# A hybrid decoder trunk on one core: attention operands in 128-row operations placed by two transfers in a row, logits copied with values, one norm step moved ahead, and one weight granule taken off priority

## The chip, the core and the metric

The kernel runs on one core of one Trainium2 chip. The metric is the device time of one execution in microseconds (us). Three runs of the kernel before took 1808.95, 1806.12 and 1806.35 us; the median is 1806.35 us. The kernel works throughout on fp32 data, 512 tokens (T) of width 1024.

## The reference, cut to what matters

```python
for l in range(DEPTH):                                    # DEPTH = 2
    x = x + 0.5 * swiglu(rms_norm(x, ffn1_norm[l]), ffn1_w_in[l], ffn1_w_out[l])
    h = rms_norm(x, mix_norm[l]) @ w_mix_in[l]
    (c_x, c_b, c_c, h_q, h_f, h_i, h_g, f_q, f_k, f_v, f_f) = jnp.split(h, split_at, axis=-1)
    y = jnp.concatenate([
        short_conv_mixer(c_x, c_b, c_c, conv_w[l]),       # 256 channels
        hgrn2_mixer(h_q, h_f, h_i, h_g, lower_bounds[l], hgrn_out_gain[l]),   # 4 heads of 64
        fox_mixer(f_q, f_k, f_v, f_f, fox_f_bias[l], fox_q_gain[l], fox_k_gain[l]),  # 8 heads of 64
    ], axis=-1)
    x = x + y @ w_mix_out[l]
    x = x + 0.5 * swiglu(rms_norm(x, ffn2_norm[l]), ffn2_w_in[l], ffn2_w_out[l])
```

In `fox_mixer` queries and keys are RMS-normed per head; the score of query t and key s gets `c_t - c_s`, where c is the running sum of `log_sigmoid(f_f + f_bias)`; then a causal mask, a softmax and the product with the values. In `hgrn2_mixer` the output of the recurrence is RMS-normed per head and multiplied by a gate.

## The kernel before

**Products in parts.** Each fp32 product is made of three matmuls on a high and a low part of both operands (`mm3`, L322, L330, L331). Weights stream through `granule`: SyncE issues the load of a tile `st` (L294, two buffers), ScalarE casts it to the high part of a tile `hl` (L311), VectorE subtracts to get the low part (L312; three `hl` buffers). These two casts normally have high priority in the scheduler, which puts the instructions of each engine into one order by priorities and readiness. An engine runs its instructions strictly in that order.

**PSUM.** There are eight banks: three called mm, two sc, two pt, one po. A tile of a name waits until the readers of the tile that had the bank before it are done.

**The mixing stage** (`mix`, L1023, once a layer) projects, then runs three mixers beside each other. The last projection before the recurrence gives the HGRN values and the eight forgetting logits in one product 264 wide, in four banks of 128 tokens: ScalarE copies 256 columns to `v` (L1122), VectorE makes the logits `zf` from the other 8 (L1125), four of each. The generator `hgrn` ends with its norm: two matmuls sum squares into two pt banks (`mb`, L1463), then come Ln, Exp and Square on ScalarE, and a Newton step of which the first two VectorE operations (L1473, `T<-pt,T`, one per half of the tile) read the two banks again and so give them back. L1476 to L1485 finish the output `hy`.

**Attention.** `fox_prep` makes a head's operands: four TensorE transposes (L1560) bring 64 query rows and 64 key rows into one bank; for the heads 0 and 1 it is an sc bank, for all others a pt bank. The score is a product over 128 + 66 rows: KA with QA, and KB with QB. QA holds the high query part in rows 0 to 63 and the low one in rows 64 to 127; KA holds the high key part in both halves; QB holds the high query part and two rows of ones, KB the low key part and two rows of the sums c. ScalarE writes QA's upper half (L1563) and KA's lower half (L1564), SyncE copies QB from QA and KA from KA (L1565, L1566, 64 rows, 128 KB each), VectorE writes QA's lower half (L1567) and KB (L1571). GpSimd fills QB's ones (L1557), SyncE loads KB's sums (L1556).

`fox_attend` goes over the items (head, query block i). `scores` runs three items ahead (`LOOK`): two matmuls into an sc bank (L1586, L1587), a custom VectorE operation for mask and maximum (L1591), Exp, reciprocal (L1595), scaling (L1597; L1599 on VectorE for i = 2). Then the block P is transposed into a pt bank (L1651); ScalarE casts it to PH (L1653), VectorE subtracts to PL (L1654); `values` multiplies (L1609) into the po bank, which L1622 and L1623 empty. Head h+1 is prepared at item (h, 0), ahead of that item's scores; each half of four heads prepares its own first head when it starts. Heads 0 to 3 run beside the projections of the convolution (L322 `mm<-x,hl`), heads 4 to 7 beside the first part of the output projection (`most`: `hy`, `cyh`, `fyh`). The rest of the output projection (three of eight rows of tiles, in two groups `dg`) follows; in each group the first granule is 128x1024.

The times below are of layer one; layer two runs the same program about 892 us later.

Of the kernel before, what the change touches and what calls it, by code (L numbers as in the profile page):

```python
# [8 lines left out]
F32 = mybir.dt.float32  # L9
F32R = mybir.dt.float32r  # L10
# [3 lines left out]
AF = mybir.ActivationFunctionType  # L14
# [9 lines left out]
P = 128  # L24
# [133 lines left out]
class Trunk:  # L158
# [177 lines left out]
        for _ in self.stream_steps(*args, **kw):  # L336
            pass

    def stream_steps(self, jobs, parts_of, act, nk, mid=None, pre=None, given=None, queued=False, ending=None):
        k = 0  # L340
        while k < nk:
            kk = min(2, nk - k)
            if callable(mid) and k == nk - 2:
                mid()
            if pre is not None:
                pre(k)
            end = k + kk == nk
            if end and ending is not None:
                jobs = ending
            skew = SKEW_MOVING if jobs[0][2] is not None and jobs[-1][0].shape[-1] < T else 0  # L350
            keep = given is not None and given(k)
            rows = self.granule(
                parts_of(k, kk), kk, pre is None, skew, keep, queued, queued and k == 0
            )
            if keep:
                yield
            order = (
                [(job, j) for job in jobs for j in range(kk)]
                if end
                else [(job, j) for j in range(kk) for job in jobs]  # L360
            )
            for n, ((acc, cols, toks, *more), j) in enumerate(order):
                if pre is not None and n == len(order) // 2:
# [659 lines left out]
    def mix(self, l, w, w_out, conv_w, out_gain, q_gain, k_gain, f_bias, next_gain):  # L1023
# [3 lines left out]
        with tc.tile_pool(name=self.n("mix"), bufs=1) as mp:  # L1027
# [88 lines left out]
                [(bv[i][:, :264], slice(0, 264), TOK[i]) for i in range(4)],  # L1116
                cols((H_I, 256), (F_F, 8)), self.xact, KD,
            )
            v = hp.tile([P, 4, 256], F32, tag="v", name=self.n("v"))
            zf = mp.tile([P, 4, NH], F32, tag="zf", name=self.n("zf"))  # L1120
            for i in range(4):
                nc.scalar.activation(  # L1122
                    v[:, i, :], bv[i][:, :256], AF.Copy, scale=self.invc[:, i : i + 1]
                )
                nc.vector.scalar_tensor_tensor(  # L1125
                    out=zf[:, i, :], in0=bv[i][:, 256:264], scalar=self.invc[:, i : i + 1],
                    in1=fb, op0=ALU.mult, op1=ALU.add,
                )
            half = [{}, {}]

            def projections():
# [6 lines left out]
            for part, n in enumerate(hgrn):  # L1138
                if n is None:
                    break  # L1140
                if n == 0:
                    left.close()
                    ap1 = left.enter_context(
                        tc.tile_pool(name=self.n("at"), bufs=1, reuse_waits="tile")
                    )
                    for tag in ("PH", "PL"):
                        ap1.tile([P, 4, 2, P], F32R, tag=tag, name=self.n(tag), bufs=2)
                    ops = {h: self.fox_prep(ap1, h, half[0][0], qkg, "sc") for h in range(2)}
                if part < 2:
# [3 lines left out]
            attend = self.fox_attend(ap1, 0, half[0], qkg, ops)  # L1153
            next(attend)
            for _ in dense:
                pass
# [41 lines left out]
            def rows(k0, a, n):  # L1198
                return lambda k, kk: [
                    w_out[order[k0 + k] * P : (order[k0 + k] + kk) * P, a : a + n]  # L1200
                ]
# [15 lines left out]
                        add(2 * dg + i, banks[i])  # L1217

            beside(attend, conv(), 1, finish)
            beside(self.fox_attend(ap1, 1, half[1], qkg, {}), most())  # L1220
            self.ntog = 0
            for dg in range(2):
                banks = self.next4()
                self.stream(
                    [(bk, c, None) for bk, c in zip(banks, TOK)],
                    rows(5, 512 * dg, 512), act(5), 3,
                )
                for i in range(4):
                    j = 4 * dg + i
                    add(j, banks[i])  # L1230
                    self.norm_part(j, ap2)
# [33 lines left out]
    def hgrn(self, l, hp, hb, z, q, v, sg, og):  # L1265
# [202 lines left out]
        for x in range(2):  # L1468
            self.act(span(r, x), mb[x], AF.Ln, bias=self.epsc)
        self.act(r, r, AF.Exp, scale=-0.5)  # L1470
        self.act(t, r, AF.Square)
        for x in range(2):
            nc.vector.scalar_tensor_tensor(  # L1473
                out=span(t, x), in0=mb[x], scalar=EPS, in1=span(t, x), op0=ALU.add, op1=ALU.mult
            )
        nc.vector.tensor_scalar(t, t, scalar1=-0.5, scalar2=1.5, op0=ALU.mult, op1=ALU.add)  # L1476
        nc.vector.tensor_mul(r, r, t)
        nc.vector.tensor_mul(o, o, r)
# [70 lines left out]
                )  # L1549
        half[hf] = qk, V  # L1550

    def fox_prep(self, pool, h, qk, g, tag="pt"):
        nc = self.nc
        tl = lambda p, tag: pool.tile([p, T], F32R, tag=tag, name=self.n(tag), bufs=2)
        QA, QB, KA, KB = tl(P, "QA"), tl(66, "QB"), tl(P, "KA"), tl(66, "KB")
        nc.sync.dma_start(KB[64:66, :].bitcast(F32), self.negc[h : h + 1, :, :].bitcast(F32))  # L1556
        nc.gpsimd.memset(QB[64:66, :].bitcast(F32), 1.0)  # L1557
# [6 lines left out]
        nc.scalar.activation(KA[64:, :], b[64:, :], AF.Copy, scale=g[64:, :])  # L1564
        nc.sync.dma_start(QB[:64, :].bitcast(F32), QA[:64, :].bitcast(F32))  # L1565
# [8 lines left out]
        )  # L1574
        return QA, QB, KA, KB

    def fox_attend(self, pool, hf, qkv, g, ops):
        nc = self.nc
        qk, V = qkv
# [52 lines left out]
        if heads[0] not in ops:  # L1632
            ops[heads[0]] = self.fox_prep(pool, heads[0], qk, g)
# [239 lines left out]
```

## Time and profile before

| | |
|---|---|
| runs, us | 1808.95, 1806.12, 1806.35 |
| median, us | 1806.35 |
| profiled execution, us | 1808.44 |
| its span, us | 1806.7 |
| TensorE (PE) busy | 1795.8 us, 99% |
| VectorE (DVE) busy | 1453.4 us, 80% |
| ScalarE (ACT) busy | 1000.7 us, 55% |
| GpSimd (POOL) busy | 170.4 us, 9% |
| granted TensorE clock | full in all 40 slices |

The profiled execution is 1.74 us longer than its span and 2.1 us longer than the median. A row of the timeline gives the start, the time to the modelled end and, in brackets, the idle time ahead of it with the instruction that ended it. Matmuls overlap in the pipeline, so that a row's second column is longer than what the matmul costs; what TensorE loses is read from the distance of two starts. VectorE's and ScalarE's rows overlap a little in the same way.

### The profile page before, as it was taken

What the parts mean: (1) busy time and instruction counts of PE and PEld (TensorE: products, weight loads), DVE (VectorE), ACT (ScalarE), POOL (GpSimd) and SP (SyncE); (2) the same over time, 40 slices, a digit from 0 to 9 for tenths busy, and PEclk for the clock granted to TensorE, in tenths of its full rate; (3) what the DMA queues carried; (4) which work ended last, traced back from release to release, by engine and by line L of the source; (5) the groups of instructions that cost most, each with busy time, mean ns of one, the idle gap of its engine ahead of it and who ended that gap; (6) DMA issues with size and microseconds to landing.
All of it is one profiled execution on the core that took longest, in us unless ns stands there. A gap on an engine that the chain in (4) does not pass through costs nothing.

```text
span 1806.7 us, 34748 instructions
## 1 busy us (share of the span) xinstructions
PE 1795.8 (99%) x14267; PEld 1681.3 (93%) x14267; DVE 1453.4 (80%) x2036; ACT 1000.7 (55%) x1437; POOL 170.4 (9%) x172
## 2 busy tenths in 40 slices
PE   9999999999999999999999999999999999999999
PEld 7899999899888899999889999998998888999997
DVE  8889787776887898879679887876868878888893
ACT  5455554464786465556446555555547855555551
POOL 0011120100000001112001111201000000020210
PEclk9999999999999999999999999999999999999999
DMA  7668783233323767868265787823333247687762
GB/s 203 182 142 186 178 178 98 72 79 83 88 74 111 218 140 161 198 160 169 82 205 133 165 189 191 169 66 81 78 89 89 71 138 188 164 159 192 159 134 94
DMA packets 243486, 250.94 MB, mean 139 GB/s; under 512 B 18520, under 2 KB 228192, under 8 KB 243328
## 3 DMA queue, kind: packets, MB, share of 16 engines
q1 hardware_dynamic: 189424, 182.38, 33.8%
q0 software_dynamic: 53600, 66.09, 23.2%
q8 instruction: 112, 1.84, 0.4%
q14 instruction: 46, 0.38, 0.1%
q10 hardware_dynamic: 304, 0.27, 0.0%
HBM read 223.98 MB, written 2.10 MB: 125 GB/s over the span
## 4 chain that ended last, share of the span: by engine, by line
PE 92%; DVE 3%; ACT 3%; issue 1%; DMA 1%; SPq 0%; ACTq 0%; DVEq 0%
PE mm L322 13%; PE mm L330 13%; PE mm L331 13%; PE sc L330 6%; PE sc L331 6%; PE sc L322 6%; PE pt L322 6%; PE pt L330 6%; PE pt L331 6%; PE po L330 4%; PE po L322 4%; PE po L331 4%; ACT hl L311 1%; PE po L1609 1%; PE pt L1651 1%
## 5 line engine op out<-in xcount | busy, mean ns | idle before, releaser
L803 ACT CAST hl<-w 128x1024 fp32r<-128x1024 f32 x322 | 336.7, 1050 | 313.7 <-PE mm L331 82.4
L805 DVE TENSOR_TENSOR hl<-w,hl 128x1024 fp32r<-128x1024 f32 x322 | 392.2, 1221 | 80.7 <-ACT hl L803 80.7
L312 DVE TENSOR_TENSOR hl<-st,hl 128x512 fp32r<-128x512 f32 (+3 forms) x192 | 162.3, 845 | 106.3 <-ACT hl L311 105.5
L311 ACT CAST hl<-st 128x512 fp32r<-128x512 f32 (+3 forms) x192 | 142.6, 743 | 169.9 <-PE po L331 64.6
L322 PE MATMUL mm<-xc,hl 128*128 128x256 f32 (+1 forms) x733 | 201.2, 276 | 0.0
L330 PE MATMUL mm<-xc,hl 128*128 128x256 f32 x728 | 201.2, 276 | 0.0
L331 PE MATMUL mm<-xc,hl 128*128 128x256 f32 x728 | 201.0, 276 | 0.0
L322 PE MATMUL sc<-xc,hl 128*128 128x256 f32 (+1 forms) x532 | 146.0, 276 | 0.0
L330 PE MATMUL sc<-xc,hl 128*128 128x256 f32 x528 | 146.0, 276 | 0.0
L331 PE MATMUL sc<-xc,hl 128*128 128x256 f32 x528 | 145.9, 276 | 0.0
L322 PEld LDWEIGHTS mm<-xc,hl 128*128 128x128 f32 x733 | 137.4, 188 | 0.2
L330 PEld LDWEIGHTS mm<-xc,hl 128*128 128x128 f32 x728 | 136.7, 188 | 0.0
L331 PEld LDWEIGHTS mm<-xc,hl 128*128 128x128 f32 x728 | 136.7, 188 | 0.0
L322 PE MATMUL pt<-xc,hl 128*128 128x256 f32 (+1 forms) x482 | 132.6, 276 | 0.0
L330 PE MATMUL pt<-xc,hl 128*128 128x256 f32 x480 | 132.6, 276 | 0.0
L331 PE MATMUL pt<-xc,hl 128*128 128x256 f32 x480 | 132.5, 276 | 0.0
L322 PE MATMUL mm<-x,hl 128*128 128x512 f32 x272 | 107.4, 395 | 0.0
L331 PE MATMUL mm<-x,hl 128*128 128x512 f32 x272 | 106.4, 391 | 0.0
L330 PE MATMUL mm<-x,hl 128*128 128x512 f32 x272 | 106.1, 390 | 0.0
L322 PEld LDWEIGHTS sc<-xc,hl 128*128 128x128 f32 x532 | 99.7, 188 | 0.2
L331 PEld LDWEIGHTS sc<-xc,hl 128*128 128x128 f32 x528 | 99.1, 188 | 0.1
L330 PEld LDWEIGHTS sc<-xc,hl 128*128 128x128 f32 x528 | 99.2, 188 | 0.0
(513 smaller groups left out, 5594.1 us busy)
## 6 DMA issues: line engine op xcount, KB each, us to landing
w<-in_ffn_w_in_dram SPq DMA_DIRECT2D x140, 512.0 KB
w<-in_ffn_w_out_dram SPq DMA_DIRECT2D x64, 512.0 KB
w<-in_ffn_w_out_dram POOLq DMA_DIRECT2D x56, 512.0 KB, 8.3
st<-in_w_mix_in_dram SPq DMA_DIRECT2D x88, 256.0 KB
st<-in_ffn_w_in_dram SPq DMA_DIRECT2D x70, 256.0 KB
w<-in_ffn_w_in_dram POOLq DMA_DIRECT2D x35, 512.0 KB, 8.5
w<-S POOLq DMA_DIRECT2D x35, 512.0 KB, 4.7
st<-in_ffn_w_out_dram SPq DMA_DIRECT2D x24, 512.0 KB
```

What stands on the lines that cost most here:

```text
L311: a = nc.scalar.copy(hi, src[:, c : c + w])
L312: b = nc.vector.tensor_sub(lo, src[:, c : c + w], hi)
L322: i = nc.tensor.matmul(acc[:, c], ah, bh[:, c], start=first and c.start == 0, stop=False, skip_group_check=True,)
L330: nc.tensor.matmul(acc, a, b, start=False, stop=False, skip_group_check=True)
L331: i = nc.tensor.matmul(acc, c, d, start=False, stop=last, skip_group_check=True)
L803: A(nc.scalar.copy(hi, src))
L805: return lambda: V(nc.vector.tensor_sub(lo, src, hi))
L1609: nc.tensor.matmul(self.ob[:, t0 + u * P : t0 + 2 * P], V[:, j, h % 4].rearrange("p a d -> p (a d)"), part[:, j, u:, :].rearrange("p i t - ...
L1651: nc.tensor.transpose(tb[:, j * P : (j + 1) * P], p[:, j * P : (j + 1) * P], self.ident)
```

## The change

It has five parts.

1. `v` is 264 wide. ScalarE copies the logits with the values, and one VectorE addition makes all of `zf`.
2. Heads 2 to 7 are prepared in a new way: ScalarE writes 128 rows (KA) in one operation, VectorE 128 rows (QA) in one. Each then holds one half where it belongs and one that belongs elsewhere; SyncE moves the high queries to QB and the low keys to KB, and then GpSimd's queue moves KA's lower half to its upper half and QB's rows into QA's lower half. The second pair needs the first. Heads 0 and 1 keep the old way. QB is two tiles that stay, whose ones are filled once a layer.
3. Head h+2 is prepared at item (h, 0), after that item's scores; so the heads 4 and 5 are prepared while the first half runs.
4. Square and the two operations that read `mb` get high priority.
5. The first granule of the last stream (`dg` 0) loses it (`calm`), and is cast in two pieces.

```diff
@@ stream_steps
-                parts_of(k, kk), kk, pre is None, skew, keep, queued, queued and k == 0
+                parts_of(k, kk), kk, pre is None and not (calm and k == 0), skew, keep,
+                queued, queued and k == 0,
@@ mix
-            v = hp.tile([P, 4, 256], F32, tag="v", name=self.n("v"))
+            v = hp.tile([P, 4, 264], F32, tag="v", name=self.n("v"))
...
-                    v[:, i, :], bv[i][:, :256], AF.Copy, scale=self.invc[:, i : i + 1]
-                )
-                nc.vector.scalar_tensor_tensor(
-                    out=zf[:, i, :], in0=bv[i][:, 256:264], scalar=self.invc[:, i : i + 1],
-                    in1=fb, op0=ALU.mult, op1=ALU.add,
-                )
+                    v[:, i, :], bv[i][:, :264], AF.Copy, scale=self.invc[:, i : i + 1]
+                )
+            nc.vector.tensor_add(
+                zf, v[:, :, 256:264], fb.unsqueeze(1).to_broadcast([P, 4, NH])
+            )
...
+                    self.qb = pair(ap1, "QB", F32R)
+                    for t in self.qb:
+                        nc.gpsimd.memset(t[64:66, :].bitcast(F32), 1.0)
...
-                    rows(5, 512 * dg, 512), act(5), 3,
+                    rows(5, 512 * dg, 512), act(5), 3, calm=dg == 0,
@@ hgrn
-        self.act(t, r, AF.Square)
-        for x in range(2):
-            nc.vector.scalar_tensor_tensor(
-                out=span(t, x), in0=mb[x], scalar=EPS, in1=span(t, x), op0=ALU.add, op1=ALU.mult
-            )
+        with self.tc.high_priority():
+            self.act(t, r, AF.Square)
+            for x in range(2):
+                nc.vector.scalar_tensor_tensor(
+                    out=span(t, x), in0=mb[x], scalar=EPS, in1=span(t, x),
+                    op0=ALU.add, op1=ALU.mult,
+                )
@@ fox_prep
+        if second is not None:
+            row = lambda a, x: a[64 * x : 64 * x + 64, :].bitcast(F32)
+            nc.scalar.activation(KA, b, AF.Copy, scale=g)
+            nc.vector.scalar_tensor_tensor(
+                out=QA, in0=b, scalar=g, in1=KA, op0=ALU.mult, op1=ALU.subtract
+            )
+            nc.sync.dma_start(row(QB, 0), row(KA, 0))
+            nc.sync.dma_start(row(KB, 0), row(QA, 1))
+            second.dma_start(row(KA, 0), row(KA, 1))
+            second.dma_start(row(QA, 1), row(QB, 0))
+            return QA, QB, KA, KB
@@ fox_attend
-            if i == 0 and h + 1 in heads and h + 1 not in ops:
-                ops[h + 1] = self.fox_prep(pool, h + 1, qk, g)
...
+            if i == 0 and h + 2 < NH:
+                ops[h + 2] = self.fox_prep(
+                    pool, h + 2, half[(h + 2) // 4][0], g, second=nc.gpsimd
+                )
```

Lines behind the change move down by up to 16 (L1473 becomes L1477, L1560 L1565, L1586 L1602, L1591 L1607, L1609 L1625, L1651 L1666, L1654 L1669).

**The norm's end on VectorE**, layer one. Before, the first operation that reads an `mb` bank (`T<-pt`) stands behind two of the four low parts of V, and the second behind the mask-and-maximum of the next block (`P,nm<-sc`) and a PL:

```order
L312 TENSOR_TENSOR hl_5573<-st_5570,hl_5573 128x512
L1546 SCALAR_TENSOR_TENSOR V_5246<-mm_5247,invc_3890,V_5246 128x4x64
L1546 SCALAR_TENSOR_TENSOR V_5246<-po_5248,invc_3890,V_5246 128x4x64
L1473 SCALAR_TENSOR_TENSOR T_5544<-pt_5376,T_5544 128x512
L1546 SCALAR_TENSOR_TENSOR V_5246<-mm_5247,invc_3890,V_5246 128x4x64
L312 TENSOR_TENSOR hl_5608<-st_5605,hl_5608 128x512
L1546 SCALAR_TENSOR_TENSOR V_5246<-po_5248,invc_3890,V_5246 128x4x64
L1591 ISA P_5476,nm_5474<-sc_5471,zm_3700 128x512
L1591 ISA nm_5474 128x1
L1654 TENSOR_TENSOR PL_5482<-pt_5483,PH_5481 128x128
L1473 SCALAR_TENSOR_TENSOR T_5544<-pt_5377,T_5544 128x512
```

With the change both stand ahead of V, with one granule's low part between them:

```order
L1607 ISA P_5404,nm_5402<-sc_5399,zm_3700 128x384
L1607 ISA nm_5402 128x1
L1611 RECIPROCAL rs_5383<-rs_5383 128x1
L1611 RECIPROCAL rs_5393<-rs_5393 128x1
L1477 SCALAR_TENSOR_TENSOR T_5556<-pt_5373,T_5556 128x512
L312 TENSOR_TENSOR hl_5585<-st_5582,hl_5585 128x512
L1477 SCALAR_TENSOR_TENSOR T_5556<-pt_5374,T_5556 128x512
L1611 RECIPROCAL rs_5403<-rs_5403 128x1
L1551 SCALAR_TENSOR_TENSOR V_5243<-mm_5244,invc_3890,V_5243 128x4x64
L1615 TENSOR_SCALAR P_5404<-P_5404,rs_5403 128x384
```

Behind these, head 2's new operation (`QA<-pt,qkg,KA`) has joined VectorE, after the rest of V and the mask-and-maximum:

```order
L312 TENSOR_TENSOR hl_5620<-st_5617,hl_5620 128x512
L1551 SCALAR_TENSOR_TENSOR V_5243<-mm_5244,invc_3890,V_5243 128x4x64
L1551 SCALAR_TENSOR_TENSOR V_5243<-po_5245,invc_3890,V_5243 128x4x64
L1607 ISA P_5473,nm_5471<-sc_5468,zm_3700 128x512
L1607 ISA nm_5471 128x1
L1571 SCALAR_TENSOR_TENSOR QA_5478<-pt_5482,qkg_3704,KA_5479 128x512
L1669 TENSOR_TENSOR PL_5494<-pt_5495,PH_5493 128x128
```

So the reads of `mb` moved ahead of all of V, and a whole head's preparation came in behind them; before, it stood some 50 TensorE rows later.

**TensorE at the same place.** Before, the scores of head 0 (its last) and head 1 (its first), then the transpose of the first block P, then the convolution's projection:

```order
L1586 MATMUL sc_5471<-KA_5286,QA_5284 128x512
L1587 MATMUL sc_5471<-KB_5287,QB_5285 128x512
L1586 MATMUL sc_5487<-KA_5303,QA_5301 128x128
L1587 MATMUL sc_5487<-KB_5304,QB_5302 128x128
L1651 MATMUL pt_5483<-ident,P_5387 128x128
L322 MATMUL mm_5451<-x_383_3562,hl_5505 128x512
```

With the change head 2's four transposes (L1565) go ahead of P's; they take the first of the two pt banks that `mb` held, and P's transpose the second:

```order
L1602 MATMUL sc_5468<-KA_5286,QA_5285 128x512
L1603 MATMUL sc_5468<-KB_5287,QB_5281 128x512
L1565 MATMUL pt_5482<-ident,qk_4132 128x128 x4
L1666 MATMUL pt_5495<-ident,P_5384 128x128
L1602 MATMUL sc_5499<-KA_5301,QA_5300 128x128
L1603 MATMUL sc_5499<-KB_5302,QB_5282 128x128
```

Twelve projection matmuls later the next P transpose (`pt_5509`, x2) takes the bank that head 2's transposes fill.

**TensorE where the halves meet**, layer one. Before, head 4 is prepared when the first half is nearly done, right behind the last P transposes of head 3, and head 5 directly after; the scores of head 4 come some 20 rows later:

```order
L1651 MATMUL pt_6044<-ident,P_5991 128x128 x4
L1560 MATMUL pt_6070<-ident,qk_4812 128x128 x4
L322 MATMUL mm_6159<-cyh_3698,hl_6203 128x512
L1609 MATMUL po_6039<-PH_6031,V_4603 128x256
L330 MATMUL mm_6159<-cyl_6017,hl_6203 128x512
```

With the change the heads 4 and 5 have been prepared, and at that place stand the transposes of head 6 in two pieces, with head 4's third and fourth scores among them:

```order
L1666 MATMUL pt_6067<-ident,P_5999 128x128 x4
L1565 MATMUL pt_6131<-ident,qk_4809 128x128 x2
L1602 MATMUL sc_6107<-KA_5828,QA_5827 128x384
L1603 MATMUL sc_6107<-KB_5829,QB_5281 128x384
L1602 MATMUL sc_6117<-KA_5828,QA_5827 128x512
L1625 MATMUL po_6062<-PH_6054,V_4600 128x256
L1603 MATMUL sc_6117<-KB_5829,QB_5281 128x512
L1565 MATMUL pt_6131<-ident,qk_4809 128x128 x2
```

So the scores of the second half moved ahead of the output projection's `cyh` products. GpSimd's queue has twelve transfers more a layer and six fills fewer; SyncE's queue has the same number of transfers.

More of the change, by code (lines that the diff above doesn't have):

```diff
@@ L337, in stream, with stream_steps @@
             pass
-    def stream_steps(self, jobs, parts_of, act, nk, mid=None, pre=None, given=None, queued=False, ending=None):
+    def stream_steps(self, jobs, parts_of, act, nk, mid=None, pre=None, given=None, queued=False, ending=None, calm=False):
         k = 0
@@ L1152, in mix @@
                     next(dense, None)
-            attend = self.fox_attend(ap1, 0, half[0], qkg, ops)
+            attend = self.fox_attend(ap1, 0, half, qkg, ops)
             next(attend)
@@ L1219, in mix @@
             beside(attend, conv(), 1, finish)
-            beside(self.fox_attend(ap1, 1, half[1], qkg, {}), most())
+            beside(self.fox_attend(ap1, 1, half, qkg, ops), most())
             self.ntog = 0
@@ L1550, in fox_qkv, with fox_prep @@
         half[hf] = qk, V
-    def fox_prep(self, pool, h, qk, g, tag="pt"):
+    def fox_prep(self, pool, h, qk, g, tag="pt", second=None):
         nc = self.nc
         tl = lambda p, tag: pool.tile([p, T], F32R, tag=tag, name=self.n(tag), bufs=2)
-        QA, QB, KA, KB = tl(P, "QA"), tl(66, "QB"), tl(P, "KA"), tl(66, "KB")
+        QA, KA, KB = tl(P, "QA"), tl(P, "KA"), tl(66, "KB")
+        QB = self.qb[h % 2][:66, :]
         nc.sync.dma_start(KB[64:66, :].bitcast(F32), self.negc[h : h + 1, :, :].bitcast(F32))
-        nc.gpsimd.memset(QB[64:66, :].bitcast(F32), 1.0)
         b = self.bank(tag)
@@ L1575, in fox_prep, with fox_attend @@
         return QA, QB, KA, KB
-    def fox_attend(self, pool, hf, qkv, g, ops):
+    def fox_attend(self, pool, hf, half, g, ops):
         nc = self.nc
-        qk, V = qkv
+        V = half[hf][1]
         tl = lambda tag, n: pool.tile([P, T], F32, tag=tag, name=self.n(tag), bufs=n)
```

2 lines of the change are left out of this document (removed).

## The prediction

> **What bounds the kernel now.** I read the page's first and fourth parts first.
>
> ```profile
> PE 1795.8 (99%) x14267; PEld 1681.3 (93%) x14267; DVE 1453.4 (80%) x2036; ACT 1000.7 (55%) x1437; POOL 170.4 (9%) x172
> PE 92%; DVE 3%; ACT 3%; issue 1%; DMA 1%; SPq 0%; ACTq 0%; DVEq 0%
> ```
>
> TensorE is busy throughout and makes up 92% of the chain that ended last. Matmuls and transposes are not changed by the edit, so it can only win or lose where TensorE waits. Next I grouped TensorE's instructions by line.
>
> ```profile
> L1651 PE MATMUL pt<-ident,P 128*128 128x128 f32 x160 | 28.2, 276 | 3.3 <-DVE T L1473 2.6 <-DVE KB L1571 0.4
> ```
>
> The last column is idle time: 2.6 us over both layers wait for L1473, which gives back the norm's banks, 0.4 for a head's KB. Since the pipeline hides the beginning of a wait, idle understates the loss. So I went through TensorE's timeline and took the distance of two starts, less the usual one: 0.06 us for a product 128 wide, 0.12 for 256 (the first row below, to the second, is longer by a wait), 0.23 for 512 (525.38 to 525.61 further down).
>
> **The waits that stand in the change's way**, each as the last row before it and the first after it. The logits:
>
> ```profile
> 383.24 0.28 PE L330 MATMUL mm<-hl,x 128*128 128x256 f32 x1
> 383.36 0.28 PE L331 MATMUL mm<-hl,x 128*128 128x256 f32 x1
> 384.02 0.38 PE L322 MATMUL mm<-hl,x 128*128 128x256 f32 x1 [0.38 <-DVE zf L1125]
> 383.25 0.46 ACT L1122 ACTIVATE v<-mm,invc 128x256 f32<-128x256 f32 x1
> 383.74 0.23 DVE L1125 SCALAR_TENSOR_TENSOR zf<-mm,invc,fb 128x8 f32<-128x8 f32 x1 [0.89 <-ACT v L1122]
> ```
>
> The bank now comes free at the end of zf, 383.97; with the logits copied by ScalarE it comes free at the end of `v`, 383.71. Gain 0.25 us in layer one; I count none in layer two. The three removed zf operations a layer lie on VectorE beside TensorE's work and count nothing.
>
> The norm's banks, layer one and two:
>
> ```profile
> 470.27 0.28 PE L1587 MATMUL sc<-KB,QB 66*128 66x128 f32 x1
> 472.08 0.33 PE L1651 MATMUL pt<-ident,P 128*128 128x128 f32 x1 [1.53 <-DVE T L1473]
> 1362.87 0.28 PE L1587 MATMUL sc<-KB,QB 66*128 66x128 f32 x1
> 1364.24 0.33 PE L1651 MATMUL pt<-ident,P 128*128 128x128 f32 x1 [1.10 <-DVE T L1473]
> ```
>
> Excess 1.81 - 0.06 = 1.75 and 1.37 - 0.06 = 1.31 us.
>
> A head's turn, and a PL that is late where VectorE has a head's operands to make in two operations of 64 rows:
>
> ```profile
> 487.35 0.39 PE L322 MATMUL mm<-x,hl 128*128 128x512 f32 x1
> 487.92 0.41 PE L1651 MATMUL pt<-ident,P 128*128 128x128 f32 x2 [0.18 <-DVE KB L1571]
> 506.67 0.36 PE L1609 MATMUL po<-PH,V 128*128 128x256 f32 x1
> 507.16 0.38 PE L1609 MATMUL po<-PL,V 128*128 128x256 f32 x1
> L1567 DVE SCALAR_TENSOR_TENSOR QA<-pt,qkg,QA 64x512 fp32r<-64x512 f32 x12 | 8.9, 744 | 2.3 <-ACT KA L1564 2.1
> L1473 DVE SCALAR_TENSOR_TENSOR T<-pt,T 128x512 f32<-128x512 f32 x4 | 2.7, 686 | 0.4 <-ACT T L274 0.4
> ```
>
> 0.57 - 0.23 = 0.34 and 0.49 - 0.12 = 0.37. A 64-row operation takes 744 ns, and the 128-row form of the same instruction at L1473 686, so a head costs VectorE one operation in place of two, some 0.8 us less, and ScalarE one less too. This shortens the queue ahead of each PL. I take both waits as gone.
>
> Where the halves meet, and in the second half:
>
> ```profile
> 520.13 0.48 PE L322 MATMUL mm<-cyh,hl 128*128 128x512 f32 x1
> 520.62 0.39 PE L1609 MATMUL po<-PH,V 128*128 128x256 f32 x1
> 525.38 0.39 PE L330 MATMUL mm<-fyl,hl 128*128 128x512 f32 x1
> 525.61 0.40 PE L331 MATMUL mm<-fyh,hl 128*128 128x512 f32 x1
> 526.32 0.44 PE L1586 MATMUL sc<-KA,QA 128*128 128x384 f32 x1 [0.32 <-DVE nm L1591]
> 536.68 0.39 PE L331 MATMUL mm<-cyh,hl 128*128 128x512 f32 x1
> 537.20 0.41 PE L1651 MATMUL pt<-ident,P 128*128 128x128 f32 x2
> 552.08 0.36 PE L1609 MATMUL po<-PH,V 128*128 128x256 f32 x1
> 552.61 0.39 PE L1609 MATMUL po<-PL,V 128*128 128x256 f32 x1 [0.17 <-DVE PL L1654]
> ```
>
> 0.26 + 0.48 + 0.29 = 1.03 where two heads are prepared in a row, which no longer happens, and 0.53 - 0.12 = 0.41 at the late PL.
>
> Layer one sums to 0.25 + 1.75 + 0.34 + 0.37 + 1.03 + 0.41 = 4.15. For layer two I take the same but for the rows that I have: 1.31 + 0.34 + 0.37 + 1.03 + 0.41 = 3.46. **Removed: 7.6 us.**
>
> **What takes their place.** The moved Square and the operations behind it:
>
> ```profile
> 467.72 0.79 ACT L1597 ACTIVATE P<-P,rs 128x128 f32<-128x128 f32 x2
> 470.25 1.05 ACT L274 ACTIVATE T<-T 128x1024 f32<-128x1024 f32 x1
> 470.28 0.48 DVE L1546 SCALAR_TENSOR_TENSOR V<-mm,invc,V 128x256 fp32r<-128x256 f32 x1
> 470.67 0.48 DVE L1546 SCALAR_TENSOR_TENSOR V<-po,invc,V 128x256 fp32r<-128x256 f32 x1
> 473.32 0.68 DVE L1591 CUSTOM_DVE_ANT_0 P<-sc,zm 128x512 f32<-128x512 f32 x1
> 473.93 0.08 DVE L1591 DVE_READ_ACCUMULATOR2_ANT nm<- 128x1 f32 x1
> ```
>
> Square (470.25) goes behind the first of the two P operations at 467.72, so from about 468.1 to 469.1. A VectorE operation on 128x512 comes every 0.6 us (473.32 to 473.93), a V every 0.39. The first T then runs to 469.7, the granule's low part to 470.3, the second T to 470.9. TensorE ends the scores at 470.2, needs the first bank (free), does head 2's four transposes (0.36) and asks for the second bank at 470.55. Wait: 0.4 in layer one; in layer two, where the present wait is 0.44 shorter, none.
>
> The next wait is new. After the second T VectorE has a reciprocal (0.1), four V (4 x 0.39), the 128x384 scaling (0.35), a low part (0.6), the mask-and-maximum (0.6), and only then head 2's QA (0.62): 470.95 + 0.1 + 1.56 + 0.35 + 0.6 + 0.6 + 0.62 = 474.8. TensorE, after P's transpose at 470.95, the scores 128 wide and 12 matmuls of 0.23, wants that bank for the next P transpose at 473.95. Wait: **0.85 us** in layer one, 0.8 in layer two, and for head 3, by the same count, 0.13 in each. Behind QA on VectorE stands the PL of the first block, whose own bank is wanted 0.6 us later; nothing there adds.
>
> Where the halves meet, head 5's transposes now stand ahead of this row, and its QA behind a 256-wide low part, a convolution operation and the mask-and-maximum:
>
> ```profile
> 514.36 0.27 PE L1651 MATMUL pt<-ident,P 128*128 128x128 f32 x1
> 514.54 0.42 DVE L312 TENSOR_TENSOR hl<-st,hl 128x256 fp32r<-128x256 f32 x1
> ```
>
> 514.54 + 0.34 + 3 x 0.6 = 516.7. TensorE is at the next P transpose after four transposes (0.36), one (0.09), eight products (0.84), head 4's first scores (0.35) and a matmul (0.23): 516.2, wait some 0.3 to 0.5. A little later the third score wants an sc bank that the mask-and-maximum at about 520.4 gives back, TensorE being there at 520.2. I take 0.3 + 0.17; the ends are none, and the 1.03 that stands there now. No row of before shows these waits, so all the new ones are held between 0 and twice my sum.
>
> **New: 0.4 + 0.85 + 0.13 + 0.47 = 1.85, and 0.8 + 0.13 + 0.47 = 1.4. Together 3.25.**
>
> **The two transfers in a row.** The old pair of transfers goes out at once, the new goes one after the other.
>
> ```profile
> 521.88 0.47 SPq L1566 DMA_DIRECT2D KA<-KA  x1
> 524.40 0.22 PE L1586 MATMUL sc<-KA,QA 128*128 128x128 f32 x1
> w<-S POOLq DMA_DIRECT2D x35, 512.0 KB, 4.7
> ```
>
> KA<-KA is read 2.5 us after its issue, so one leg lasts at most 2.5; two legs 5. A GpSimd transfer here takes 4.7 from issue to landing for four times the bytes, which bounds the second leg from above. Head 5 has least time: QA at 516.7, first leg at 519.3 at latest, second at 521.9 (as SyncE's) or 524.1 (as w<-S). Its first score, by counting the rows ahead of it, is due at about 522.5. The other heads have over ten microseconds. I take the 2.5 (the same kind of move, the same bytes): no cost; with 4.7 it is 1.6 us a layer. SyncE's queue waits for QA before it moves on to the next `st`; those loads run two granules ahead, so 0 to 0.5, taken as 0. GpSimd has nothing else in this stage than the fills.
>
> [...]
>
> **Calm** changes nothing I can count.
>
> ```profile
> 564.36 0.39 PE L1609 MATMUL po<-PH,V 128*128 128x256 f32 x1 [0.41 <-ACT PH L1653]
> ```
>
> This wait comes from PH behind a 128x1024 cast on ScalarE; the new order keeps the second group's cast, with high priority, ahead of that PH. At the first group's granule TensorE doesn't wait now.
>
> **Sum.** 7.6 - 3.25 = 4.4 us. Against the profiled execution 1808.44 that is 1804.0; this execution is 2.1 above the median, and nothing says that the excess is in these stages, so I take 4.4 off the median 1806.35: **1802.0 us**, 0.24%. About 0.2%, 3.6 us, is what a measurement of this kernel can tell from no change.
>
> **The rivals.**
> ```profile
> 475.00:500.00 25.00, 24.82 (x138) 20.81 (x137) 22.82 (x52) 19.53 (x44) 1.05 (x2) 1.00 0.31 78
> ```
>
> This row gives busy time in 25 us of the first half: TensorE 24.82, loads 20.81, VectorE 22.82, ScalarE 19.53.
>
> - *The banks return late at every head* (slower). Twelve preparations (heads 2 to 7, two layers) hold one of only two pt banks until ScalarE and VectorE are both done. VectorE is busy 22.82 of 25 us there, so an operation put before QA delays it in full. My waits are 3.25 over 12, 0.27 each. From 7.6 / 12 = 0.63 on average the change costs more than it brings, and from 0.93 it is slower by 3.6; at one 128x512 operation and one 256 more ahead of each QA, 1.0 us, it gives 12 - 7.6 = 4.4 more, 1810.8. For it speaks the wait at 487.92, against it that the old form held the same bank for two operations. Chance 0.17.
> - *GpSimd's leg is late* (4.7 us): 2 x 1.6 = 3.2 of the 4.4 are lost, 1805.2. For it speaks the only GpSimd row, against it its four times larger transfer. Chance 0.08.
> - *Square only moves the wait*: its 1.05 us on ScalarE delays Exp and V, and TensorE loses it at the next P transpose, once a layer: 4.4 - 2.1 = 2.3, 1804.05. Against it: that transpose follows 12 matmuls, 2.7 us later. Chance 0.10.
> - *Lighter*: the new waits are half as long, and calm ends the 0.41 in both layers (that it doesn't do what it says is my forecast): 4.4 + 1.6 + 0.8 = 6.8, 1799.5. Chance 0.10.
> - *The forecast*, 1802.0, between 1799.9 and 1804.4 as the unknown waits go: 0.55, of which 0.40 below 1802.75 (0.2% faster) and 0.15 above.
>
> **The numbers.** Faster: 0.40 + 0.10 = 0.50. Same: 0.15 + 0.08 + 0.10 = 0.33. Slower: 0.17. The range leaves the slower rival out: from 1798.7 (all 7.6 gained, no new wait) to 1806.5 (twice the new waits, 1805.25, and GpSimd's leg with part of its 3.2).
>
> **What the changed profile would show.** The rows on L1473's successor and KB among TensorE's waits go; in their place a wait of 0.4 at the first P transpose and one of 0.8 to 0.9, ended by QA, at the next. Head 5's first score follows the matmul ahead of it without a wait; if it waits for a transfer, the second rival holds. Idle time ended by QA, summed over the transposes, above 7 us shows the first. The wait at 563.55 stays. I would be wrong most of all in the order of VectorE's work between 469 and 475, on which the largest gain and the largest new wait both rest.

## The result and the profile after

The changed kernel takes 1804.46 us (median of 14 runs, 1802.93 to 1806.13), the kernel before 1807.37 (14 runs); the ratio is 0.9982, interval 0.9975 to 0.9989. By the ratio it is 3.3 us faster (2.0 to 4.5), where 4.35 was forecast. The forecast's absolute time, 1802.0, is 2.5 us too low; 1.0 of these come from its base, the median of three runs, 1806.35.

The page after, its first and fourth parts, and TensorE's costliest waits as the view of waits has them (total, times, longest), before and after:

```profile
PE 1796.0 (100%) x14267; PEld 1683.9 (93%) x14267; DVE 1442.3 (80%) x2020; ACT 992.8 (55%) x1427; POOL 176.9 (10%) x184
PE 93%; DVE 2%; ACT 2%; DMA 1%; issue 1%; SPq 0%; ACTq 0%; DVEq 0%
```

```profile
PE pt L1651 <- DVE T L1473: 2.6, 2, 1.5
...
PE po L1609 <- ACT PH L1653: 0.8, 2, 0.4
PE sc L1586 <- DVE nm L1591: 0.7, 2, 0.4
PE pt L1651 <- DVE KB L1571: 0.4, 2, 0.2
PE mm L322 <- DVE zf L1125: 0.4, 1, 0.4
```

```profile
PE pt L1666 <- DVE QA L1571: 1.3, 2, 0.7
...
PE po L1625 <- ACT PH L1668: 1.0, 2, 0.5
```

The 2.6 us for the norm's banks are gone, and so are the waits for KB and nm; half of the 2.6 has come back as the wait for QA, and the wait for PH has grown a little. To see gains and losses by place I count TensorE's matmuls in order of start (14267 in each kernel) and take two stretches a layer: the **front** (matmul 2700 to 3940, and 9800 to 11066: the last projections and the recurrence) and the **attention** (3940 to 4700, and 11066 to 11826, from ahead of the norm's end until well after the mixing stage).

| us | before | after | after - before |
|---|---|---|---|
| front, layer one and two | 83.40, 85.97 | 83.81, 86.39 | +0.83 |
| attention, layer one and two | 148.71, 148.20 | 146.50, 146.04 | -4.37 |
| sum | 466.28 | 462.74 | -3.54 |

The profiled executions differ by less, 1808.44 and 1806.13, because TensorE's 300th matmul starts at 68.45 us before and 69.88 after. That is not the change's: over the other twelve profiles, whose opening is the same, this start lies between 67.2 and 70.1.

TensorE's timeline after, at the norm's end and the next P, layer one:

```profile
472.02 0.60 PE L1565 MATMUL pt<-ident,qk 128*128 128x128 f32 x4
472.61 0.30 PE L1666 MATMUL pt<-ident,P 128*128 128x128 f32 x1
...
475.50 0.39 PE L331 MATMUL mm<-x,hl 128*128 128x512 f32 x1
476.53 0.41 PE L1666 MATMUL pt<-ident,P 128*128 128x128 f32 x2 [0.65 <-DVE QA L1571]
```

and VectorE beside it:

```profile
474.63 0.48 DVE L1551 SCALAR_TENSOR_TENSOR V<-po,invc,V 128x256 fp32r<-128x256 f32 x1
475.03 0.68 DVE L1607 CUSTOM_DVE_ANT_0 P<-sc,zm 128x512 f32<-128x512 f32 x1
475.64 0.08 DVE L1607 DVE_READ_ACCUMULATOR2_ANT nm<- 128x1 f32 x1
475.64 0.75 DVE L1571 SCALAR_TENSOR_TENSOR QA<-pt,qkg,KA 128x512 fp32r<-128x512 f32 x1
476.30 0.28 DVE L1669 TENSOR_TENSOR PL<-pt,PH 128x128 fp32r<-128x128 f32 x1
```

The second bank costs 0.59 - 0.36 = 0.2 us; QA costs 1.03 - 0.23 = 0.8, in layer two the same. VectorE goes from V to the mask-and-maximum to QA without a gap. QA is done where PL starts, 476.30, and TensorE starts 0.2 us later.

The logits, where the front loses:

```profile
384.79 0.28 PE L331 MATMUL mm<-hl,x 128*128 128x256 f32 x1
385.24 0.39 PE L322 MATMUL mm<-hl,x 128*128 128x256 f32 x1 [0.18 <-ACT v L1123]
...
387.42 1.04 PE L1315 MATMUL pt<-ident,T 128*128 128x128 f32 x8
388.55 0.40 PE L1510 MATMUL sc<-utri,flh 128*8 128x512 f32 x1
```

The wait for the bank shrank from 0.54 to 0.33 us. But the eight transposes, which took 0.84 before, are followed after 1.13, so TensorE now waits 0.3 for `flh`, the operand of the decay's first sum, which is the next link that hangs on the same ScalarE operation (Exp, then v, then zf, then the decay). The 0.2 was given back three microseconds later.

### The profile page after: what moved, and what is told of

Read it like the earlier page. It is cut to its first block, busy times and chain, and to the rows that moved or that the text cites. A ratio compares the mean times of both kernels' runs of the same rounds, so it can differ in the third digit from the quotient of the medians.

```text
span 1804.4 us, 34742 instructions
## 1 busy us (share of the span) xinstructions
PE 1796.0 (100%) x14267; PEld 1683.9 (93%) x14267; DVE 1442.3 (80%) x2020; ACT 992.8 (55%) x1427; POOL 176.9 (10%) x184
## 4 chain that ended last, share of the span: by engine, by line
PE 93%; DVE 2%; ACT 2%; DMA 1%; issue 1%; SPq 0%; ACTq 0%; DVEq 0%
PE mm L322 13%; PE mm L331 13%; PE mm L330 13%; PE sc L330 6%; PE sc L322 6%; PE sc L331 6%; PE pt L322 6%; PE pt L330 6%; PE pt L331 6%; PE po L331 3%; PE po L322 3%; PE po L330 3%; PE po L1625 1%; PE pt L1666 1%; DMA st<-in_ffn_w_in_dram 1%
```

## The experiments

Each ratio is against the kernel before, with its interval. The two right columns are the stretches of the profiled executions, layers one and two.

| kernel | ratio | front | attention |
|---|---|---|---|
| changed | 0.9982 (0.9975 to 0.9989) | 83.81, 86.39 | 146.50, 146.04 |
| a_logits_alone | 1.0007 (0.9998 to 1.0016) | 83.63, 86.37 | 148.27, 148.19 |
| b_old_logits | 0.9979 (0.9968 to 0.9989) | 83.37, 85.95 | 146.66, 146.02 |
| c_wide_tile | 1.0004 (0.9995 to 1.0013) | 83.57, 86.39 | 148.23, 148.26 |
| g_qa_priority | 0.9982 (0.9973 to 0.9991) | 83.59, 86.39 | 146.36, 146.18 |
| i_prep_later | 0.9982 (0.9973 to 0.9992) | 83.57, 86.39 | 146.48, 146.13 |
| d_no_priority | 0.9987 (0.9978 to 0.9997) | 83.38, 85.77 | 146.97, 146.56 |
| j_old_form | 1.0020 (1.0010 to 1.0029) | 83.24, 85.77 | 150.56, 149.79 |
| p_old_time | 1.0082 (1.0059 to 1.0106) | 83.27, 86.39 | 151.38, 153.98 |
| q_old_form_old_time | 1.0002 (0.9993 to 1.0011) | 83.84, 86.39 | 148.57, 147.51 |
| e_sync_leg | 0.9986 (0.9977 to 0.9996) | 83.39, 86.38 | 146.79, 146.60 |
| f_no_calm | 0.9983 (0.9974 to 0.9992) | 83.41, 86.39 | 146.47, 146.18 |
| m_best | 0.9973 (0.9963 to 0.9983) | 82.77, 86.01 | 146.49, 146.06 |

The intervals are some 3.5 us wide, so for terms under a microsecond the stretches of the traces decide; the front of layer one moves by up to 0.6 from trace to trace, since ScalarE reaches the four copies to `v` up to 0.55 us earlier or later beside TensorE.

### Where the front's 0.8 us go: the logits' part

Three kernels. The first is the kernel before with the logits' part alone, the second the changed kernel without it:

```diff
-            v = hp.tile([P, 4, 256], F32, tag="v", name=self.n("v"))
+            v = hp.tile([P, 4, 264], F32, tag="v", name=self.n("v"))
...
+            nc.vector.tensor_add(
+                zf, v[:, :, 256:264], fb.unsqueeze(1).to_broadcast([P, 4, NH])
+            )
```

> The kernel before with the logits' part of the change alone (v 264 wide, one addition for zf). The changed kernel wins 4.5 us in the two attention stages of its profile, as forecast (4.4), but loses some 1.0 us ahead of them. Theory A: that loss belongs to the logits' part. Then this kernel alone is 0.7 to 1.2 us slower than before (+0.04 to 0.07%), the 256-wide matmuls of the projections between 436 and 454 us start every 118 ns where before has 113, and the first sum of the decay (sc<-utri,flh) waits 0.2 to 0.3 us in layer one, while the 0.55 us wait for zf falls to 0.34. Rival B: the loss belongs to other parts or to the execution that was profiled; then this kernel is 0 to 0.3 us faster than before and the pace stays at 113 ns.

> The changed kernel with the old logits (v 256 wide, four VectorE operations for zf); all else as changed, TensorE's order the same. Theory A: the loss ahead of the attention stages goes, and the gain over before is 4.0 to 4.7 us (ratio 0.9974 to 0.9978). Rival B: it stays, ratio 0.9980 to 0.9984.

The third is the kernel before with only the tile's width changed; ScalarE and VectorE still use 256 columns and the four old zf:

```diff
-            v = hp.tile([P, 4, 256], F32, tag="v", name=self.n("v"))
+            v = hp.tile([P, 4, 264], F32, tag="v", name=self.n("v"))
...
-                    v[:, i, :], bv[i][:, :256], AF.Copy, scale=self.invc[:, i : i + 1]
+                    v[:, i, :256], bv[i][:, :256], AF.Copy, scale=self.invc[:, i : i + 1]
```

> The kernel before with the tile v made 264 wide and nothing else: every engine's order is that of before, only the places of tiles in memory differ. Theory A1: the slower pace of the projections (118 against 113 ns) is one of the places; then it shows here too, and the kernel is 0.5 to 0.9 us slower than before. Theory A2: it comes from the work beside, so 113 ns stay and the time is that of before to 0.2 us.

Measured: the front of the second kernel is back at 83.37 and 85.95, and that of the first and third at 86.4 in layer two. The second kernel's ratio, 0.9979, lies between the two ranges that were expected, and its interval covers both, so the stretches decide: theory A and A1 hold. Layer two shows it plainly, 85.97 and 85.95 with the narrow tile and 86.39 with the wide one: 0.42 us, all of it the tile's width, since c_wide_tile changes nothing else. In layer one c_wide_tile lost only 0.17, because the wait for zf was shorter in its execution (0.19 us of idle for 0.38). The 40 matmuls around that wait (2740 to 2780) take 5.50 us in before and 5.26 in c_wide_tile, both with the old logits, and 5.49 in the changed kernel, 5.27 and 5.25 in g and i, all with the new ones: the one addition for zf gains nothing there. Seven matmuls in a row, of before and of c_wide_tile:

```profile
440.83 0.28 PE L331 MATMUL mm<-hl,x 128*128 128x256 f32 x1
...
441.51 0.28 PE L331 MATMUL mm<-hl,x 128*128 128x256 f32 x1
```

```profile
440.73 0.28 PE L331 MATMUL mm<-hl,x 128*128 128x256 f32 x1
...
441.44 0.28 PE L331 MATMUL mm<-hl,x 128*128 128x256 f32 x1
```

Six starts take 0.68 us in the one (113 ns each) and 0.71 in the other (118). Over this stretch (144 products a layer, between 436 and 456 us in before) the mean is 113.5 and 117.8 ns, in both layers and in every kernel: 113.5 in the three with the narrow tile (before, b, m), 117.8 in the eleven with the wide one, whatever else they change. The next 48 products of the same kind go the other way, 117.8 ns with the narrow tile and 113.5 with the wide one. So the wide tile costs 0.58 us a layer and gives back 0.2, the most of it still in the front.

### The wait for QA: bank or backlog

```diff
-            nc.scalar.activation(KA, b, AF.Copy, scale=g)
-            nc.vector.scalar_tensor_tensor(
-                out=QA, in0=b, scalar=g, in1=KA, op0=ALU.mult, op1=ALU.subtract
-            )
+            with self.tc.high_priority():
+                nc.scalar.activation(KA, b, AF.Copy, scale=g)
+                nc.vector.scalar_tensor_tensor(
+                    out=QA, in0=b, scalar=g, in1=KA, op0=ALU.mult, op1=ALU.subtract
+                )
```

> The changed kernel with high priority for the two operations that make a head's operands (KA on ScalarE, QA on VectorE). On VectorE head 2's QA goes ahead of one V and the mask-and-maximum, 1.0 us earlier. If the forecast's new wait is what it was said to be (the pt bank held until QA), the waits of 0.81 us in both layers go to 0 and the gain over before is 1.4 to 1.8 us larger than the changed kernel's 2.9 to 3.3 (ratio 0.9972 to 0.9975). Rival: what is moved behind QA (mask-and-maximum, PL) makes TensorE wait in its place, and the ratio stays at 0.9980 to 0.9984.

Neither. QA moved ahead by 1.0 us or a little more on VectorE, and on TensorE the scheduler put P's transpose ahead by five matmuls (1.15 us) as well, presumably because it counted on the bank earlier. Both sides moved, so this run doesn't tell the bank from the backlog. The wait stayed:

```profile
471.33 0.39 PE L322 MATMUL mm<-x,hl 128*128 128x512 f32 x1
472.34 0.44 PE L1667 MATMUL pt<-ident,P 128*128 128x128 f32 x2 [0.62 <-DVE QA L1572]
```

Then head 2 one item later, so that it holds another bank:

```diff
-            if i == 0 and h + 2 < NH:
+            if i == (h == 0) and h + 2 < NH:
```

> The changed kernel with head 2 prepared one item later, so that its transposes stand behind the first P transpose and head 1's first scores; nothing else is moved by hand. Theory A (TensorE waits because head 2 holds the bank that the second P needs): the second P takes the other bank, and the 0.81 us in both layers go to 0.2 or less. Theory B (TensorE waits for VectorE's backlog; which bank is handed over last doesn't matter, since the first block's PL stands behind the same V and mask-and-maximum): a wait of 0.5 to 0.9 us stays at the second or third P, ended by PL or QA.

```profile
472.29 0.39 PE L322 MATMUL mm<-x,hl 128*128 128x512 f32 x1
473.20 0.30 PE L1666 MATMUL pt<-ident,P 128*128 128x128 f32 x1 [0.52 <-DVE PL L1669]
```

0.91 - 0.23 = 0.68 us, now ended by PL: theory B. VectorE has a backlog here (four V, a granule's low part, a mask-and-maximum), and TensorE waits for its end, whichever instruction hands the bank over: QA in the changed kernel (0.8 us), PL here (0.68). No run here makes the backlog itself shorter, so that the wait would then go is not shown.

### The norm's priority

```diff
-        with self.tc.high_priority():
+        if True:
             self.act(t, r, AF.Square)
```

> The changed kernel without the high priority of the norm's Square and of the two operations that read the norm's banks. Theory A (the priority is what took the norm's wait away): TensorE waits 1.4 to 1.8 us in layer one and 1.1 to 1.6 in layer two for the first operation that reads the banks, now at head 2's transposes; since QA comes after that wait anyway, its 0.81 us go, so the two attention stages of the trace are 1 to 2 us longer together than those of the changed kernel. Rival B (the wait went because head 2's transposes and the new order moved the place where it is felt): under 0.4 us of difference.

The waits are back, at head 2's transposes (2.1 us of idle in the view of waits, against 1.3 for QA), and the attention is 0.47 + 0.52 = 1.0 us longer: theory A, at its lower end. By start distances the two waits are 1.3 and 1.2 us, the first a little under what was expected, and QA's are gone. Layer two's front is shorter here by 0.62 because its first projections ran at 113 ns a matmul; so the kernel as a whole shows less.

```profile
PE pt L1565 <- DVE T L1477: 2.1, 2, 1.1
```

### Form and time of the heads' preparation

The old form at the new time, and the new form at the old time:

```diff
-                    pool, h + 2, half[(h + 2) // 4][0], g, second=nc.gpsimd
+                    pool, h + 2, half[(h + 2) // 4][0], g
```

> The changed kernel with its new time of preparation but the old form for all heads (two operations of 64 rows on ScalarE and two on VectorE, both transfers of SyncE at once, none of GpSimd). Theory A (the form carries the waits at a head's turn and at late PLs, 0.34 + 0.37 + 0.41 a layer, the time of preparation the others): the two attention stages are 1.5 to 2.5 us longer together than the changed kernel's, with the waits on KB and PL back. Theory B (the time of preparation alone does it): within 0.5 us.

```diff
-            beside(self.fox_attend(ap1, 1, half, qkg, ops), most())
+            beside(self.fox_attend(ap1, 1, half, qkg, {}), most())
...
+        if heads[0] not in ops:
+            ops[heads[0]] = self.fox_prep(pool, heads[0], qk, g, second=nc.gpsimd)
...
+            if i == 0 and h + 1 in heads and h + 1 not in ops:
+                ops[h + 1] = self.fox_prep(pool, h + 1, qk, g, second=nc.gpsimd)
...
-            if i == 0 and h + 2 < NH:
-                ops[h + 2] = self.fox_prep(
-                    pool, h + 2, half[(h + 2) // 4][0], g, second=nc.gpsimd
-                )
```

So the preparation stands ahead of the item's scores as before, and head 4 is prepared at the start of its half.

> The changed kernel with the new form but the old time of preparation: head h+1 at item (h, 0), head 4 when the second half starts. In the traces so far the two attention stages together last 296.9 us before, 292.5 changed, and 300.4 with the old form at the new time. Theory A (form and time need each other: two transfers in a row last some 5 us, which the old time doesn't cover at head 4): where the halves meet head 4's first score waits 1.5 to 3 us a layer for a transfer, and the stages last 295 to 298 us. Theory B (the form alone carries the gain, the time nothing): 292.0 to 293.5 us, and no wait for a transfer.

And neither, only the other three parts on the kernel before:

> The kernel before with the three parts of the change that don't touch the heads' preparation: logits with values, the norm's priority, calm. Theory A (the norm's wait of 1.75 and 1.31 us goes, all waits at the heads stay): the two attention stages last 293.8 to 294.8 us. Theory B (the priority only moves VectorE's backlog on to the next waits, as high priority for QA did): 295.5 to 296.9 us.

| attention, both layers, us | old time | new time |
|---|---|---|
| old form | 296.1 | 300.4 |
| new form | 305.4 | 292.5 |

Before itself lasts 296.9. Both theories A were right in kind and far too small in size. **The old form at the new time** is 7.8 us longer than the changed kernel, 3.4 longer than before. Its waits, and the busy times in 30 us of the first half (stretch, length, then TensorE, weight loads, VectorE, ScalarE, GpSimd), there and in the changed kernel:

```profile
PE pt L1666 <- DVE KB L1587: 2.8, 6, 0.7
...
PE pt L1666 <- ACT P L1613: 0.6, 2, 0.3
PE pt L1666 <- DVE PL L1669: 0.6, 2, 0.3
```

```profile
470.00:500.00 30.00, 29.11 (x156) 23.72 (x155) 28.09 (x65) 23.89 (x52) 0.00 (x0) 1.00 0.33 89
```

```profile
470.00:500.00 30.00, 29.35 (x156) 24.53 (x155) 26.83 (x63) 23.32 (x55) 2.13 (x4) 1.00 0.42 106
```

VectorE is 28.09 us busy of 30, against 26.83, and TensorE waits six times for KB, which the second VectorE operation of the old form writes. **The new form at the old time** waits for the second leg:

```profile
PE sc L1602 <- DMA QA<-QB: 8.3, 6, 2.8
```

```profile
489.32 0.28 PE L1625 MATMUL po<-PL,V 128*128 128x128 f32 x1
491.94 0.30 PE L1602 MATMUL sc<-KA,QA 128*128 128x128 f32 x1 [2.35 <-DMA QA<-QB]
```

not mainly at head 4, as expected, but most of all at head 2 (here, and 3.05 us by start distances in layer two), and at the heads 3 and 5 as well. Its 8.5 us over before are not all waits. After the 2.84 us of idle at head 2 in layer two TensorE's granted clock stands at half for 3.4 us, from 1389.0 to 1392.4, as this row shows (TensorE's clock is the third number from the end):

```profile
1390.00:1392.00 2.00, 2.00 (x7) 1.52 (x6) 0.00 (x0) 0.33 (x1) 0.00 (x0) 0.50 0.00 0
```

That is some 1.7 us lost, an estimate from half of 3.4. The 2.35 us of idle in layer one had no such stretch behind it. This kernel's four runs took 1815.57, 1816.56 (the profiled one), 1825.35 and 1825.46 us, with mean granted clocks of 0.999, 0.999, 0.995 and 0.994, so that its ratio, 1.0082, is larger than what its trace shows (8.5 us are 0.5%).

**Neither** is 0.8 us better than before, theory B; 0.87 of what is missing is a weight tile that came late in this one execution (ScalarE's cast at 562.72 idles 0.77 for it), so the priority is worth between 0.8 and 1.7 without the new preparation, not the 3.06 of the waits that it ends.

### GpSimd's legs

```diff
-                    pool, h + 2, half[(h + 2) // 4][0], g, second=nc.gpsimd
+                    pool, h + 2, half[(h + 2) // 4][0], g, second=nc.sync
```

> The changed kernel with both legs of the transfers on SyncE's queue. The legs land 2.2 to 2.9 us after issue in the changed kernel and no first score of a head waits. Theory A (the GpSimd leg costs nothing, its place is hidden): the attention stages stay within 0.3 us; the second leg issued by SyncE lands after 2.2 to 2.3 us. Theory B (GpSimd's legs are late, or SyncE's queue would be blocked by the waiting legs): for the first, 0.5 us or more shorter; for the second, weight tiles come late and TensorE waits for hl, 0.5 us or more longer.

Transfers by queue, KB each and us to landing, in the changed kernel and in this one:

```profile
QB<-KA SPq DMA_DIRECT2D x12, 128.0 KB, 2.2
KB<-QA SPq DMA_DIRECT2D x12, 128.0 KB, 2.3
KA<-KA POOLq DMA_DIRECT2D x12, 128.0 KB, 2.2
QA<-QB POOLq DMA_DIRECT2D x12, 128.0 KB, 2.9
```

```profile
KA<-KA SPq DMA_DIRECT2D x16, 128.0 KB, 2.4
...
QA<-QB SPq DMA_DIRECT2D x12, 128.0 KB, 2.3
```

The medians for QA<-QB are 2.3 us from SyncE and 2.9 from GpSimd. But of SyncE's twelve the trace has only three landings (2.2, 2.3 and 3.0 us), and GpSimd's twelve lie between 2.2 and 4.8, so that a difference is not shown. Nothing is gained by the other queue: the attention is 0.29 and 0.56 us longer. Of layer two's 0.56 some 0.5 goes back to a weight tile that came 0.45 later, ahead of the norm and of the first leg (ScalarE idles 1.11 for it, in the changed kernel 0.66). So the expected 0.3 is met in layer one only, together it is missed, and theory B's second half (a blocked queue) isn't shown, nor fully excluded.

### Calm

```diff
-                    rows(5, 512 * dg, 512), act(5), 3, calm=dg == 0,
+                    rows(5, 512 * dg, 512), act(5), 3,
```

> The changed kernel without calm: the first granule of the last stream is cast in one piece again, with high priority; TensorE's order the same. Theory A, as forecast: nothing, the attention stages stay at 292.2 to 292.9 us and the wait for PH behind the second group's cast stays at 0.6 to 0.7. Theory B: calm is worth something where its PL moved, 0.3 to 0.6 us a layer.

The attention lasts 146.47 and 146.18: theory A, calm is worth nothing here. The last kernel has the old logits, and calm on both groups:

```diff
-                    rows(5, 512 * dg, 512), act(5), 3, calm=dg == 0,
+                    rows(5, 512 * dg, 512), act(5), 3, calm=True,
```

> The changed kernel with the old logits and calm on both groups of the last stream. The old logits give back 0.7 us. Theory A (the wait of 0.65 us for PH comes from the 128x1024 cast ahead of it): cast in two pieces behind PH, that wait goes, and the kernel is 4.8 to 5.8 us faster than before (ratio 0.9968 to 0.9973). Theory B: the granule's second piece is then late itself and TensorE waits for hl as long; ratio 0.9975 to 0.9979.

```profile
559.34 0.40 PE L330 MATMUL sc<-fyl,hl 128*128 128x512 f32 x1
560.18 0.39 PE L1626 MATMUL po<-PH,V 128*128 128x256 f32 x1 [0.44 <-ACT PH L1669]
```

The wait of 0.6 stays (0.84 - 0.23): the cast ahead of PH takes 0.61 us for 1.05 in the changed kernel, but the scheduler put the product that needs PH two matmuls earlier. The attention equals the changed kernel's. The kernel is the fastest of all, 1802.58 us, 0.9973, through its front alone: 82.77, where the first projections of layer one ran at 113 ns as well. So its lead over b_old_logits, 0.9973 to 0.9979 and within both intervals, is not calm's.

## Why the prediction was right, point by point

- **The norm's banks**: removed, 1.75 and 1.31. The second bank costs 0.2 and 0, forecast 0.4 and 0.
- **QA**: forecast 0.85 and 0.8, measured 0.8 and 0.8, by the same chain of VectorE's operations: QA's end, 476.30, is 474.9 when the later start of 1.43 us is taken off, and 474.8 was forecast. The account of it was half right: the bank is where the wait is felt, the backlog is what it waits for (i).
- **Head 3**: forecast 0.13, measured none.
- **A head's turn and the late PLs** (0.34, 0.37, 0.41): gone. The reason given, one VectorE operation in place of two, is borne out from both sides: p_old_time, with the new form at the old time, has none of these waits, and j_old_form, with the old form at the new time, waits for KB and PL. For layer two the prediction took layer one's rows, and there it had some luck: the third wait isn't there, but one of 0.39 for `fo` is, and it went too. The size of the form as a part was not seen: without it the new time costs 3.9 us a layer.
- **Where the halves meet**: 1.03 removed and 0.47 new were forecast; the three waits that stand there now are 0.28, 0.28 and 0.30, together 0.86 a layer. The new term was mis-sized by 0.4 a layer.
- **The two legs**: cost nothing, as taken, but the working was wrong. Two legs were bounded by 5 us. At head 5 QA ends at about 517.4, GpSimd issues the second leg only at 521.03, and this transfer lands 2.2 us later, at 523.25; the first score starts at 524.06. So the legs end 5.8 us after QA, with 0.8 of slack. At head 2 the second leg took 4.8 and 4.6 us, above the 2.5 that was taken and about the 4.7 that the prediction had as its upper bound. What hid this is the earlier preparation, as p_old_time shows. GpSimd's timeline and TensorE's, changed kernel:

```profile
520.50 0.52 POOL L1576 DMA_DIRECT2D KA<-KA  x1 [13.08 <-DVE PL L1669]
521.03 0.52 POOL L1577 DMA_DIRECT2D QA<-QB  x1
```

```profile
524.06 0.30 PE L1602 MATMUL sc<-KA,QA 128*128 128x128 f32 x1
```

- **Calm**: nothing, as forecast. The wait for PH stays, 0.58 before and 0.6 to 0.7 after.
- **The logits**: this step failed. A gain of 0.25 was forecast; the bank's wait gave 0.2, the decay's first sum took it back, and the wide tile, which the prediction did not look at, slowed 144 products a layer by 4 ns each and sped up 48. Measured: 0.8 us lost over both layers, 1.1 off the forecast.
- **The rivals**: idle ended by QA is 1.3 us in all, where more than 7 was the sign of the first; no first score waits for GpSimd's leg; and at the P transpose where Square's delay was to be felt there is QA's forecast 0.8 and no more.

In the attention the forecast was 7.35 - 3.25 = 4.1 us, and 4.37 came. The new waits that are named above sum to 3.5, so the removed ones must be some 0.5 more than was counted; where that lies stays open. In the traces the whole came out 0.8 us under the forecast, 1.1 too little at the logits and 0.3 too much in the attention; that it lies as near as this is partly luck.

## What to carry to other kernels

When an engine off the critical path is nearly full, count what each of its instructions hands over: a wait that is removed by putting one instruction ahead can come back behind the instructions that were put back, here 1.3 of 2.6 us of idle, and the scheduler may move the waiting side as well, as in g_qa_priority. Two parts of a change can each lose without the other (against the kernel with neither, the attention was 4.3 us longer with the new time alone and 9.3 with the new form alone, some 1.7 of it through the halved clock) and win together (3.5 us shorter, of which 0.9 is a late weight tile in the one execution of the kernel with neither), so undo parts one at a time before a part is judged. Look ahead of the place that a change is about, too: a wider tile there cost 0.8 us, against the attention's gain of 4.4.

## What the runs showed of the hardware

The same fp32 products 128 by 256 start every 113.5 or every 117.8 ns, by stretch, and the width of a tile that they don't touch (256 or 264 columns) decides it in two neighbouring stretches of a layer, in opposite directions, with every engine's order the same (c_wide_tile): 144 products go from 113.5 to 117.8 and the next 48 from 117.8 to 113.5. Other stretches changed pace in d_no_priority, j_old_form and m_best without any change of a tile's size there. That places in memory are what matters is likely from c; which places, and why, stays open.

Between a kernel's first and last microseconds the granted TensorE clock left full in one trace alone, p_old_time's: 3.4 us at half followed an idle time of TensorE of 2.84 us, and nothing of the kind an idle time of 2.35 us. Whether the wait caused it is not shown: it is one case in one execution.
